# A DoRA linear layer on one core: the loads of blocks 0 and 4 cut into more pieces, and the multiplication by m moved ahead of the sum of squares

## The chip, the cores and the metric

The kernel runs on one core of one Trainium2 chip. The metric is the device time of one execution in microseconds (us); lower is better.

## The reference

`x` has 32,768 rows (16 x 2048) of 256 float32 numbers. `W` is 256 x 256, `lora_A` 256 x 16, `lora_B` 16 x 256, `m` has 256 numbers and `scale` is 1.0.

```python
W_adapted = W + scale * (lora_A @ lora_B)
W_norm = np.sqrt(np.sum(W_adapted ** 2, axis=0, keepdims=True) + 1e-8)
W_final = W_adapted / W_norm * m
y = x.reshape(-1, 256) @ W_final
```

Every input row is read once (33.6 MB) and every output row written once (33.6 MB).

## The kernel before, in words

**Units.** The rows are cut into 8 blocks of 4096 rows. A block is a tile of 128 partitions, in which each partition holds 32 consecutive rows of x, 32 KB that lie together in memory. A block has 8 chunks (4 rows of each partition, 512 rows, 4 KB a partition); chunks are numbered g = 0 to 63, and two chunks make a pair, p = 0 to 31. The last block is loaded and stored as two units of half a block each (16 KB a partition).

**Buffers.** There are five buffers of a block each (`x_bufs`). The output of a chunk is written into the place of its input, and stored from there. So blocks 0 to 4 are loaded without waiting, and blocks 5, 6 and 7 only when the stores of blocks 0, 1 and 2 have freed a buffer.

**SyncE (SP)** issues W's load and all loads of x: chunks 0 and 1, chunks 2 to 7, then blocks 1, 2, 3, 4. Then it waits for stores 0, 1 and 2 (L163), issues blocks 5 and 6 and the first half of block 7, waits for store 3 and issues the second half.

**GpSimd (POOL)** makes the identity and then casts x to bf16 pair by pair into two small buffers (L192). Ahead of a pair it waits for the load that the pair begins (L183), ahead of pair 0 also for the squares on VectorE (`dve` at 4), ahead of pair 15 (`REST`) for store 2, and for the transposes that free its buffer.

**TensorE (PE)** first does the preamble: it transposes A (L267), multiplies A and B (L271), sums the squares of the adapted weights down the columns with a matrix of ones (L278), and spreads m over the partitions with a matmul of one row (L283). It transposes pair 0, waits until VectorE has finished `w_final` (`dve` at 8), and releases two output buffers (`room`). Then a loop runs: transpose pair p + 1 (8 instructions, L297), then the products of pair p (2 x 8 matmuls, L311). The products of pair p thus stand behind the transposes of pair p + 1 in PE's order.

**VectorE (DVE)** adds W and the low-rank part, squares the sum (L218), copies m from PSUM (L220), multiplies it in (L223), takes the reciprocal of the norm (L226), makes `w_final` (L229), and then copies each transposed pair from PSUM to SBUF (L233). The wait ahead of L220 is for `pe` at 4, that is for the sums and for m.

**ScalarE (ACT)** loads A, B and m, takes the square root of the sums (L243), and then copies each chunk's product from PSUM to its place in x's buffer (L251). After some chunks it issues stores on its own queue, as a table written by hand says (chunk after which it is issued in brackets): block 0 (22), block 1 (23), the halves of block 2 (24), the first four chunks of block 3 one by one (27, 4 KB a partition), the rest of block 3 and blocks 4 and 5 (47), block 6 (55), and the halves of block 7 (59 and 63).

Of the kernel before, what the change touches and what calls it, by code (L numbers as in the profile page):

```python
# [11 lines left out]
def kernel(  # L12
# [10 lines left out]
    nc = tc.nc  # L23
# [19 lines left out]
    XBUFS = 5  # L43
    CH = DJ // J
# [18 lines left out]
    def sb(name, shape, dtype):  # L63
        return ctx.enter_context(nc.sbuf_tensor(name, shape, dtype))
# [10 lines left out]
    m_row = sb("m_row", [1, OUT], FP32)  # L75
    identity = sb("identity", [P, P], FP32)
    zeros = sb("zeros", [P, P], FP32)
    ones = sb("ones", [P, P], FP32)
# [18 lines left out]
    mb_ps = y_ps[1][:, 2, :]  # L97
# [3 lines left out]

    units = [(b * CH, CH) for b in range(NBLK - 1)]
    units += [(NCH - CH, CH // 2), (NCH - CH // 2, CH // 2)]
    loads = [(0, 2), (2, CH - 2)] + units[1:]
    load_of = {g: n for n, (g0, cnt) in enumerate(loads) for g in range(g0, g0 + cnt)}


# [17 lines left out]
    def sem(name):  # L125
        if name not in sems:
            sems[name] = tc.alloc_semaphore(name)
        return sems[name]
# [50 lines left out]
    ).then_inc(sem("ident"), 1)  # L179
    for p in range(NPR):  # L180
        b, c = divmod(p, PRB)
        if p == 0 or load_of[2 * p - 1] != load_of[2 * p]:
            nc.gpsimd.wait_ge(sem(f"load{load_of[2 * p]}"), 16)  # L183
        if p == 0:


            nc.gpsimd.wait_ge(sem("dve"), 4)
        if p == REST:
            nc.gpsimd.wait_ge(sem(f"store{HALF}"), 16)
        if p >= NXB:  # L190
            nc.gpsimd.wait_ge(sem("turned"), p - NXB + 1)
        nc.gpsimd.tensor_copy(  # L192
            out=xb_bufs[p % NXB][:],
            in_=x_bufs[b % XBUFS][:, 2 * c * J : 2 * (c + 1) * J, :],
        ).then_inc(sem("rounded"), 1)
# [9 lines left out]
    dv = sem("dve")  # L205
# [10 lines left out]
    ).then_inc(dv, 1)  # L216
    nc.vector.wait_ge(dv, 3)
    nc.vector.tensor_mul(out=sq[:], in0=wa[:], in1=wa[:]).then_inc(dv, 1)  # L218
    nc.vector.wait_ge(sem("pe"), 4)
    nc.vector.tensor_copy(out=m_all[:], in_=mb_ps).then_inc(dv, 1)  # L220
    nc.vector.wait_ge(dv, 5)
    for t in range(KC):
        i = nc.vector.tensor_mul(out=wam[:, t], in0=wa[:, t], in1=m_all[:])  # L223
# [3 lines left out]
    nc.vector.wait_ge(dv, 7)  # L227
    for t in range(KC):
        i = nc.vector.tensor_mul(out=w_final[:, t], in0=wam[:, t], in1=rnorm[:])  # L229
    i.then_inc(dv, 1)  # L230
    for p in range(NPR):
        nc.vector.wait_ge(sem("turned"), p + 1)
        nc.vector.tensor_copy(  # L233
# [5 lines left out]
    nc.scalar.wait_ge(dv, 1)  # L239

    nc.scalar.activation(out=warm[:], in_=eps_col[:], func=AF.Sqrt)  # L241
    nc.scalar.wait_ge(sem("pe"), 3)
    nc.scalar.activation(  # L243
        out=norm[:], in_=n2_ps, func=AF.Sqrt, bias=eps_col[:]
    ).then_inc(sem("act"), 1)
# [1 line left out]
    for g in range(NCH):  # L247
        b, c = divmod(g, CH)
# [14 lines left out]
    pe = sem("pe")  # L263
    nc.tensor.wait_ge(sem("ident"), 1)
    nc.tensor.wait_ge(sem("load_a"), 16)
    for t in range(KC):
        i = nc.tensor.transpose(aT_ps[:, t * P : (t + 1) * P], a_nat[:, t, :], identity[:])  # L267
    i.then_inc(pe, 1)
    nc.tensor.wait_ge(dv, 2)
    for t in range(KC):  # L270
        i = nc.tensor.matmul(  # L271
            ab_ps[:, t, :], aT[:, t * P : (t + 1) * P], b_bf[:], start=True, stop=True
        )
    i.then_inc(pe, 1)
    nc.tensor.wait_ge(dv, 4)

    for t in range(KC):
        i = nc.tensor.matmul(  # L278
            n2_ps, ones[:], sq[:, t, :], start=(t == 0), stop=(t == KC - 1)
        )  # L280
    i.then_inc(pe, 1)
    nc.tensor.wait_ge(sem("load_m"), 16)
    nc.tensor.matmul(mb_ps, ones[0:1, :], m_row[:], start=True, stop=True).then_inc(pe, 1)  # L283
    def take(name):

        nc.tensor.sem_inc(sem(name), -1).wait_op(sem(name), 1, "sem-ge")  # L286
# [6 lines left out]
    def turned(p):  # L293
        take("rounded")

        for j in range(2 * J):
            i = nc.tensor.transpose(  # L297
                xt_ps[p % 2][:, j * P : (j + 1) * P],
                xb_bufs[p % NXB][:, j, :].bitcast(FP32),
                identity[:],  # L300
            )
        i.then_inc(sem("turned"), 1)
# [15 lines left out]
            i.then_inc(sem("product"), 1)  # L318

    turned(0)  # L320

    nc.tensor.wait_ge(dv, 8)
    nc.tensor.sem_inc(sem("room"), 2)
    with nc.Fori(0, NPR // 2, 1, engines=[PE], head_slot={PE: 128}):
        turned(1)
        product(0)
# [45 lines left out]
```

## Time and profile before

| | |
|---|---|
| median of 4 runs | 163.5 us (163.13 to 164.72) |
| the profiled execution's own time | 162.79 us |
| its span, from the first to the last instruction | 161.5 us |
| PE, PE weight loads, DVE, ACT, POOL busy | 60%, 52%, 28%, 40%, 39% of the span |
| moved by DMA | 67.42 MB, 418 GB/s in the mean |
| q1 (SP's queue: loads) | 33.82 MB, 49.0% of 16 engines' span |
| q10 (ACT's queue: stores, A, B, m) | 33.59 MB, 48.9% |

Busy shares are means over the whole span. A core has 16 DMA engines, which serve both queues. The page cuts the span into 40 slices of about 4 us, and gives for each slice the busy tenths of every engine, of the DMA, and the clock that TensorE was granted. Rows of the order of time give the start and the length of an instruction or of several in a row (us), the engine, the line, the tiles, and in brackets how long the engine was idle before and what ended that.

### The profile page before, as it was taken

To read this page: it belongs to the slowest core of one execution; us is meant where nothing else is said; L and a number is where in the kernel's file an instruction comes from. 1 tells how busy PE (TensorE), PEld (TensorE's weight loads), DVE (VectorE), ACT (ScalarE), POOL (GpSimd) and SP (SyncE) were. 2 spreads that over 40 slices of the span, in tenths; PEclk is the share of its full clock that TensorE was granted. 3 is DMA by queue.
4 is the path that set the end of the run, shared out by engine and by line. 5 is a ranking of instruction groups with operands and counts; after the bars stand their busy time and mean duration, and the time that the engine had idled before them with its cause. 6 is when DMAs were issued, how large, how long until landed. Compare 5 with 4: busy or idle time off the path is not lost. (4 is left out here: it accounts for less than half of the span.)

```text
span 161.5 us, 2005 instructions
## 1 busy us (share of the span) xinstructions
PE 96.8 (60%) x786; PEld 84.6 (52%) x786; DVE 44.9 (28%) x44; ACT 64.0 (40%) x67; POOL 62.7 (39%) x39
## 2 busy tenths in 40 slices
PE   0490999999999520000299979999999970000000
PEld 0251799999998310000279968989899960000000
DVE  0547335363535300000033633635353500000000
ACT  3010166868675450000026684684768680000000
POOL 1226719676863000000764449479667400000000
PEclk9999999999999975555559999999999999555555
DMA  4999999999999999999999999999999999999994
GB/s 160 465 420 457 406 503 390 406 503 390 398 511 390 390 495 390 416 430 410 442 384 419 429 449 426 407 438 418 436 463 406 471 422 398 473 430 398 430 434 199
DMA packets 3780, 67.42 MB, mean 418 GB/s; under 512 B 561, under 2 KB 578, under 8 KB 1218
## 3 DMA queue, kind: packets, MB, share of 16 engines
q1 hardware_dynamic: 1584, 33.82, 49.0%
q10 hardware_dynamic: 2194, 33.59, 48.9%
q14 instruction: 2, 0.02, 0.0%
HBM read 33.85 MB, written 33.55 MB: 417 GB/s over the span
## 5 line engine op out<-in xcount | busy, mean ns | idle before, releaser
L251 ACT COPY x_sb<-y_ps 128x1024 f32<-128x1024 f32 x64 | 62.1, 1015 | 61.9 <-PE y_ps L311 61.4
L192 POOL CAST xb<-x_sb 128x2048 bf16<-128x2048 f32 x32 | 60.2, 1893 | 62.9 <-DMA out_dram<-x_sb 27.8
L311 PE MATMUL y_ps<-w_final,xt 128*128 128x256 bf16 x512 | 64.8, 281 | 2.8 <-PEq L286 2.7
L233 DVE COPY xt<-xt_ps 128x1024 f32<-128x1024 f32 x32 | 39.2, 1224 | 76.3 <-PE xt_ps L297 76.3
L311 PEld LDWEIGHTS y_ps<-w_final,xt 128*128 128x128 bf16 x512 | 51.4, 101 | 10.8 <-issue 3.7
L297 PE MATMUL xt_ps<-identity,xb 128*128 128x128 f32 x264 | 37.3, 288 | 27.0 <-PEq L286 27.0
L297 PEld LDWEIGHTS xt_ps<-identity,xb 128*128 128x128 f32 x264 | 32.2, 149 | 29.2 <-issue 28.8
L278 PE MATMUL y_ps<-sq,ones 128*128 128x256 f32 x4 | 2.1, 674 | 1.6 <-DVE sq L218 1.6
L267 PE MATMUL y_ps<-identity,a_nat 128*16 128x128 f32 x2 | 0.6, 394 | 3.6 <-DMA a_nat<-in_lora_A_dram 3.6
L243 ACT ACTIVATE norm<-y_ps,eps_col 128x256 f32<-128x256 f32 x1 | 0.5, 473 | 5.2 <-PE y_ps L278 5.2
L278 PEld LDWEIGHTS y_ps<-sq,ones 128*128 128x128 f32 x4 | 1.2, 324 | 2.3 <-DVE sq L218 2.1
L241 ACT ACT_TABLE_LOAD x1 | 1.3, 1283 | 2.4 <-issue 2.4
L198 POOL MEMSET xb<- 128x2048 bf16 x1 | 1.8, 1804 | 0.7 <-PE xt_ps L297 0.7
L267 PEld LDWEIGHTS y_ps<-identity,a_nat 128*16 128x16 f32 x2 | 0.1, 88 | 3.6 <-issue 3.6
L226 DVE RECIPROCAL rnorm<-norm 128x256 f32<-128x256 f32 x1 | 1.7, 1745 | 0.0
L220 DVE COPY m_all<-y_ps 128x256 f32<-128x256 f32 x1 | 0.4, 425 | 3.3 <-PE y_ps L283 3.3
L283 PE MATMUL y_ps<-m_row,ones 1*128 1x256 f32 x2 | 1.2, 710 | 0.0
L209 DVE CAST b_bf<-b_nat 16x256 bf16<-16x256 f32 x1 | 0.3, 281 | 2.8 <-DMA b_nat<-in_lora_B_dram 2.8
L271 PE MATMUL y_ps<-b_bf,aT 16*128 16x256 bf16 x2 | 0.6, 404 | 0.5 <-DVE aT L211 0.5
L214 DVE SCALAR_TENSOR_TENSOR wa<-y_ps,w_nat 128x512 f32<-128x512 f32 x1 | 0.7, 690 | 0.8 <-PE y_ps L271 0.8
L283 PEld LDWEIGHTS y_ps<-m_row,ones 1*128 1x128 f32 x2 | 0.5, 308 | 0.7 <-issue 0.7
L229 DVE TENSOR_TENSOR w_final<-wam,rnorm 128x256 bf16<-128x256 f32 x2 | 0.8, 422 | 0.0
(13 smaller groups left out, 3.3 us busy)
## 6 DMA issues: line engine op xcount, KB each, us to landing
x_sb<-in_x_dram SPq DMA_DIRECT2D x6, 4096.0 KB, 29.1
out_dram<-x_sb ACTq DMA_DIRECT2D x5, 4096.0 KB, 21.3
out_dram<-x_sb ACTq DMA_DIRECT2D x5, 2048.0 KB, 27.9
x_sb<-in_x_dram SPq DMA_DIRECT2D x2, 2048.0 KB, 33.6
x_sb<-in_x_dram SPq DMA_DIRECT2D x1, 3072.0 KB, 11.8
out_dram<-x_sb ACTq DMA_DIRECT2D x4, 512.0 KB, 48.6
x_sb<-in_x_dram SPq DMA_DIRECT2D x1, 1024.0 KB, 5.0
w_nat<-in_W_dram SPq DMA_DIRECT2D x1, 256.0 KB, 2.9
```

The costliest lines, as they stand in the source:

```text
L192: nc.gpsimd.tensor_copy(out=xb_bufs[p % NXB][:], in_=x_bufs[b % XBUFS][:, 2 * c * J : 2 * (c + 1) * J, :],).then_inc(sem("rounded"), 1)
L198: nc.gpsimd.memset(xb_bufs[NPR % NXB][:], 0.0).then_inc(sem("rounded"), 1)
L214: nc.vector.scalar_tensor_tensor(out=wa[:], in0=ab_ps, scalar=float(scale), in1=w_nat[:], op0=ALU.mult, op1=ALU.add).then_inc(dv, 1)
L226: nc.vector.reciprocal(out=rnorm[:], in_=norm[:]).then_inc(dv, 1)
L229: i = nc.vector.tensor_mul(out=w_final[:, t], in0=wam[:, t], in1=rnorm[:])
L233: nc.vector.tensor_copy(out=xt_bufs[p % NXT][:].rearrange("p r t -> p (r t)").bitcast(FP32), in_=xt_ps[p % 2][:],).then_inc(sem("copied"), 1)
L241: nc.scalar.activation(out=warm[:], in_=eps_col[:], func=AF.Sqrt)
L251: nc.scalar.copy(out=x_bufs[b % XBUFS][:, c * J : (c + 1) * J, :], in_=y_ps[g % 2][:]).then_inc(sem("room"), 1)
L278: i = nc.tensor.matmul(n2_ps, ones[:], sq[:, t, :], start=(t == 0), stop=(t == KC - 1))
L283: nc.tensor.matmul(mb_ps, ones[0:1, :], m_row[:], start=True, stop=True).then_inc(pe, 1)
L297: i = nc.tensor.transpose(xt_ps[p % 2][:, j * P : (j + 1) * P], xb_bufs[p % NXB][:, j, :].bitcast(FP32), identity[:],)
L311: i = nc.tensor.matmul(y_ps[h][:, j, :], xt_bufs[p % NXT][:, r : r + P, t], w_final[:, t, :], start=(t == 0 and (j % (J // 2)) == 0), stop ...
```

## The change

- x's loads: block 0 is loaded in three pieces instead of two (chunks 0 and 1, chunks 2 and 3, chunks 4 to 7). Block 4 is loaded as its first five chunks in one piece, and its last three chunks one by one (4 KB a partition). The order of the loads stays.
- POOL waits ahead of a pair for the loads of both of its chunks, since a pair can now lie in two loads.
- On PE the matmul that spreads m comes ahead of the sum of squares. `pe` is at 3 with m and at 4 with the sums, and VectorE (m) and ScalarE (sums) wait accordingly. VectorE's copy of m and the multiplication by it can run while PE sums.
- VectorE's last instruction on `w_final` increments `room` by two itself; PE no longer stops for `w_final` ahead of its loop.

```diff
-    loads = [(0, 2), (2, CH - 2)] + units[1:]
+    loads = [(0, 2), (2, 2), (4, CH - 4)] + units[1 : XBUFS - 1]
+    loads += [((XBUFS - 1) * CH, CH - 3)]
+    loads += [(XBUFS * CH - 3 + c, 1) for c in range(3)] + units[XBUFS:]
...
-        if p == 0 or load_of[2 * p - 1] != load_of[2 * p]:
-            nc.gpsimd.wait_ge(sem(f"load{load_of[2 * p]}"), 16)
+        for g in (2 * p, 2 * p + 1):
+            if g == 0 or load_of[g - 1] != load_of[g]:
+                nc.gpsimd.wait_ge(sem(f"load{load_of[g]}"), 16)
...
-    nc.vector.wait_ge(sem("pe"), 4)
+    nc.vector.wait_ge(sem("pe"), 3)
     nc.vector.tensor_copy(out=m_all[:], in_=mb_ps).then_inc(dv, 1)
...
         i = nc.vector.tensor_mul(out=w_final[:, t], in0=wam[:, t], in1=rnorm[:])
-    i.then_inc(dv, 1)
+    i.then_inc(sem("room"), 2)
...
-    nc.scalar.wait_ge(sem("pe"), 3)
+    nc.scalar.wait_ge(sem("pe"), 4)
     nc.scalar.activation(
         out=norm[:], in_=n2_ps, func=AF.Sqrt, bias=eps_col[:]
...
+    nc.tensor.wait_ge(sem("load_m"), 16)
+    nc.tensor.matmul(mb_ps, ones[0:1, :], m_row[:], start=True, stop=True).then_inc(pe, 1)
     nc.tensor.wait_ge(dv, 4)
     for t in range(KC):
...
             n2_ps, ones[:], sq[:, t, :], start=(t == 0), stop=(t == KC - 1)
...
-    nc.tensor.wait_ge(sem("load_m"), 16)
-    nc.tensor.matmul(mb_ps, ones[0:1, :], m_row[:], start=True, stop=True).then_inc(pe, 1)
...
     turned(0)
-    nc.tensor.wait_ge(dv, 8)
-    nc.tensor.sem_inc(sem("room"), 2)
     with nc.Fori(0, NPR // 2, 1, engines=[PE], head_slot={PE: 128}):
```

## The prediction

> **What bounds the kernel now.** I read first the page's rows over 40 slices, then the DMA queues, then the order of time on PE, POOL, VectorE and ScalarE's queue at the start and at the hand-over from loads to stores, and last the granted clock in short windows.
>
> ```profile
> span 161.5 us, 2005 instructions
> PEclk9999999999999975555559999999999999555555
> DMA  4999999999999999999999999999999999999994
> q1 hardware_dynamic: 1584, 33.82, 49.0%
> q10 hardware_dynamic: 2194, 33.59, 48.9%
> ```
>
> The DMA row is full in 38 of 40 slices, and the two queues together hold 97.9% of 16 engines' span. So the end is set by the work that the 16 DMA engines have, plus any moment in which they have none; the compute engines (PE 60%) matter only where they leave the DMA without work. The profiled execution took 162.79 us, 1.3 us more than its span; the median of the four runs shown, 163.5, lies 0.7 above it.
>
> There is one place where the DMA depends on the compute. Five blocks are loaded without a pause; the loads end at 51.7 to 52.06 us by the trace's packet records, and the next work is the first store, issued after chunk 22 is evicted:
>
> ```profile
> 13.72 3.75 POOL L192 CAST xb<-x_sb 128x2048 bf16<-128x2048 f32 x2 [4.81 <-DMA x_sb<-in_x_dram]
> 23.43 5.64 POOL L192 CAST xb<-x_sb 128x2048 bf16<-128x2048 f32 x3 [3.76 <-DMA x_sb<-in_x_dram]
> 26.07 1.04 PE L297 MATMUL xt_ps<-identity,xb 128*128 128x128 f32 x8
> 48.98 1.01 ACT L251 COPY x_sb<-y_ps 128x1024 f32<-128x1024 f32 x1 [0.69 <-PE y_ps L311]
> 50.10 0.37 ACTq L145 DMA_DIRECT2D out_dram<-x_sb  x1
> ```
>
> The store is issued at 50.10 and its first packets start at 51.68, 1.58 us later: just as the loads run out. Three engines then needed 2.0 to 2.3 us for their first 32 KB store packet instead of 1.21. The hand-over has no slack; each us that chunk 22 comes later is a us of empty DMA. Chunk 22 hangs on a chain from the load of block 1: it lands at 23.4, pair 4 is cast by 25.3, and PE, which is busy all the time by then, turns pair 4 at 26.07, 0.75 us after it could have. From there PE takes 2.62 us a pair, while a block of four pairs lands every 9.75 us (2.44 a pair), so what PE loses it doesn't get back before chunk 22.
>
> After the hand-over there is cover: four MB of stores are still queued when block 5's loads are released, and the last store is issued at 133.6 while the DMA works to 161.1.
>
> **The change, part by part.**
>
> *Descriptors.* The packet records give one packet per partition row, eight a transfer on each engine: 1213 ns for 32 KB, 912 for 24 KB, 611 for 16 KB, 309 for 8 KB, 159 for 4 KB, 9 for a transfer's completion. Block 4 goes from one 32 KB row to one of 20 KB (midway, 762) and three of 4 KB: 8 x (762 + 3 x 159 - 1213) = 0.21 us for each engine. Block 0: 8 x (309 + 611 - 912) = 0.06. Four more completions: 0.04. Together 0.30 us, in full on the path, since the engines are never free. The 4 KB price is uncertain, because the trace has only 4 KB stores: 159 ns beside 32 KB loads and for the first five or so in a row, but 305 ns for some 45 of them between 81.7 and 83.1 us, just before block 5's loads join. If all 24 per engine took 305, it would be 24 x 0.146 = 3.5 us more. A gain below 159 has no row (2 KB loads take 84, which is 168 for 4 KB). I take 159: the nearest row for loads, eight 2 KB rows of W in succession, shows no such step after its first packet.
> [...]
>
> *Four more issues on SP.* 14 instead of 10, 0.43 us each, all but the last four before SP's long wait; one more lies ahead of block 1's issue, covered by block 0's 4 MB (9.7 us) in the queue. Uncovered, it would be 0.4 us of empty DMA. Block 1 lands when it did, plus 0.1.
>
> *The loads beside the stores.* Should the stores be early, the engines alternate, and each 4 KB load packet lets one 1213 ns store packet pass: 24 x 1.37 = 33 us, so chunks 37 to 39 land by some 84 us instead of 52. POOL's new wait stands before pair 18's cast (86.38 now), with all later casts behind it, and PE, VectorE and ScalarE behind those. It costs nothing, and if it were some us late, the 27 us between the last store's issue and its end would take it.
>
> *m earlier, w_final earlier.* PE's matmul for m (1.22 us at 8.94) moves ahead of the sums, into 5.4 to 6.6, where PE waits for the squares (6.94). m's last packet starts at 5.13, so m may be there a little late; up to 0.3 us could be pushed onto the sums. VectorE then copies m (0.42) and multiplies it in (0.76) from 6.9 to 8.1 instead of 10.20 to 11.4. The square root ends at 9.52, the reciprocal (1.75) at 11.3, w_final (0.76) at 12.1 instead of 13.87: 1.8 us earlier. Moving room's increment to VectorE takes PE's stop for w_final away from pair 1's transposes.
>
> *Block 0 in three.* Pair 1 waited until 13.72 for 3 MB. With 1 MB it lands some 2.4 us after the first load (6.4), at 8.9, as pair 0's cast ends. So pair 0 turns from 9.05, pair 1 from 11.0, and product 0 starts at 13.4 (w_final 12.1, pair 0's copy 1.23) instead of 17.50. Pairs 2 and 3 are cast from 13.8.
>
> So PE is 4 us ahead, and where does that go? Nothing of it reaches the DMA until pair 4, which still can't be cast before 25.3: the head start that counts is the 0.75 us of lateness above. In between PE has products 0 to 2 and pairs 2 and 3 to turn, done at 22 to 23.5, and then stands idle for 2 to 3.3 us. That is what I take to decide the case, because of PE's clock:
>
> ```profile
> 17.50 3.49 PE L311 MATMUL y_ps<-w_final,xt 128*128 128x256 bf16 x16
> 20.83 1.04 PE L297 MATMUL xt_ps<-identity,xb 128*128 128x128 f32 x8
> 21.71 1.91 PE L311 MATMUL y_ps<-w_final,xt 128*128 128x256 bf16 x16
> 58.00:60.00 2.00, 0.07 (x1) 0.00 (x0) 0.00 (x0) 1.01 (x1) 0.00 (x0) 0.57 0.95 410
> 85.00:86.00 1.00, 1.00 (x8) 1.00 (x7) 0.00 (x0) 0.79 (x1) 0.00 (x0) 0.71 0.96 410
> ```
>
> The first and third rows are the same 16 matmuls at the slow and at the full clock (pairs 5.06 and 2.62 us apart); the column before the last two is the granted clock. It rose at 20.7, 5 us after PE became steadily busy, fell at about 58.3, rose at 85.6 (5.8 us after work resumed) and fell at 136.8. These points lie on a grid of 3.41 us (27.3 is 8 steps, 51.2 is 15). It fell at 58.3 although PE had worked 1.44 of the last 3.41 us (42%); it stayed up where a 1.28 us gap left 63%. With a gap of 2 to 3.3 us at 22 to 25.4, most positions of the grid leave one step under half busy, so the clock falls, and PE works pair 4 onward slowly for 3.4 to 6 us. Slow time loses 1 - 2.62/5.06 = 48%: 1.6 to 3.0 us, less the 0.75 gained: chunk 22 comes 0.9 to 2.2 us later than in the profile. I went pair by pair through the order in the code at several positions of the grid; the middle is near the low end, 1.1 us. Of it 0.3 is absorbed, since the loads end 0.3 later, and 0.1 by the overlap of load ends: 0.7 us of empty DMA.
> [...]
>
> Sum against the profiled execution: 162.79 + 0.30 + 0.7 = 163.8. The kernel before has the same lottery: were its clock to rise one grid position later than 20.7, up to 3 us of slow time, its chunk 22 would be up to 1.5 us later, and its median is 0.7 above the profile. So I compare medians: 163.8 with 163.5, 0.2%.
>
> **The rivals.**
>
> *The clock stays up (0.24).* Then the store is issued near 49.4, 0.75 earlier, its packets run among the last 4 KB loads, and no engine is ever empty: 162.79 + 0.30 = 163.1, or 162.9 without the slow first store packets. For it: only part of the positions give a gap in one step. Against it: the row at 58.3.
>
> *The 4 KB loads stall (0.08), the slower side.* Place: 48 to 52 us, 24 packets an engine at 305 ns, 3.5 us: 166.6 with the cover above complete, since the late stores then find the loads still running. It is over 1% once 11 of 24 stall. For it: those 45 packets; against: they stand in one short stretch, and hundreds of others took 159.
>
> *A long slow stretch (0.08).* The clock stays low for two steps or more and chunk 22 is 2.5 to 3 us late: 162.79 + 0.3 + 2.4 = 165.5.
>
> *The label isn't what happens.* In my forecast the 4 KB loads end before the first store packet, so nothing runs beside anything: part of the 0.56 that I give the forecast.
>
> *Faster by over 1% (0.04)* needs 1.6 us less DMA work or gaps. The trace shows no gap of that size to remove; only runs such as the slowest before (164.72) have that much to lose.
>
> **How the numbers follow.** One per cent, 1.6 us, is about what a measurement of this kernel tells from no change. Forecast 163.8, covering 163.4 to 164.6, has 0.56. Faster by over 1%: 0.04. Slower: the stall, and half of the long stretch: 0.12. Within: 0.84. The range 162.8 to 165.4 takes in the covered hand-over and most of the long stretch, and leaves out the stall.
>
> **What would show it.** In the profile after: w_final near 12.1; product 0 near 13.4; pair 4's cast still near 23.5; before it an idle PE of 2 to 3 us, and after it 16 matmuls in 3.5 us rather than 1.9; the first store's issue after 50.1; 4 KB loads of 159 ns. It is wrong if the first store is issued before 50 (the clock held), if the 4 KB loads take 305, or if the DMA row shows a hole elsewhere.

## The result, and the profile after

| | before | after |
|---|---|---|
| median | 164.22 us (162.73 to 165.71, 63 runs) | 163.07 us (162.22 to 165.6, 42 runs) |
| runs below 162.85 / above 163.9 | 2 / 35 | 20 / 7 |
| profiled execution: own time, span | 162.79, 161.5 | 162.27, 161.0 |

The ratio after to before is 0.9941, 95% interval 0.9921 to 0.996: 0.6% faster, where +0.2% was forecast; the time itself lies in the range given. (The ratio leaves out runs over 1.5% above their kernel's fastest; the medians are over all runs.) The four runs known beforehand, median 163.5, had shown the kernel before too well: with 63 runs it is 164.2.

The page's rows of the kernel after (span; granted clock and DMA in 40 slices; the two queues' packets, MB and share):

```profile
span 161.0 us, 2011 instructions
PEclk9999699999999995555569999999999997555555
DMA  4999999999899999989999999999999999999996
q1 hardware_dynamic: 2160, 33.82, 49.3%
q10 hardware_dynamic: 2194, 33.59, 48.9%
```

The DMA still fills the span, and the loads' share has risen from 49.0% to 49.3%: the cost of the smaller descriptors. The dent of the clock in the fifth slice doesn't mean that the clock is lower there than before. The clock's records in these traces begin with its first rise, and the page shows 9 for what lies ahead of it. In the kernel before the first rise stands at 20.7, and product 0 took 3.49 us at the slow clock although its slice shows a 9. Here the clock rises at 11.9, falls at 15.3 and rises again at 18.75. Now the order of time of the kernel after, at the start and at the hand-over:

```profile
7.01 3.92 POOL L197 CAST xb<-x_sb 128x2048 bf16<-128x2048 f32 x2 [5.33 <-DVE sq L223]
...
7.95 3.25 DVE L229 TENSOR_TENSOR wam<-wa,m_all 128x256 f32<-128x256 f32 x2
...
12.90 0.76 DVE L235 TENSOR_TENSOR w_final<-wam,rnorm 128x256 bf16<-128x256 f32 x2
...
15.09 3.37 PE L318 MATMUL y_ps<-w_final,xt 128*128 128x256 bf16 x16 [2.55 <-PEq L293]
18.26 1.28 PE L304 MATMUL xt_ps<-identity,xb 128*128 128x128 f32 x8
19.38 1.91 PE L318 MATMUL y_ps<-w_final,xt 128*128 128x256 bf16 x16
...
25.53 1.06 PE L304 MATMUL xt_ps<-identity,xb 128*128 128x128 f32 x8 [1.62 <-PEq L293]
...
49.59 0.37 ACTq L149 DMA_DIRECT2D out_dram<-x_sb  x1
```

Two casts now run back to back from 7.0. The multiplication by m beside them takes 3.25 us, not 0.76, so w_final is ready at 13.66, only 0.2 earlier than before. Product 0 starts at 15.09 instead of 17.50 all the same, since pair 1's transposes were done early. Product 1, at 19.38, runs at the full clock. PE waits 1.62 us ahead of pair 4 and comes out of it at the full clock, and the first store is issued at 49.59, 0.5 us earlier than in the profile before.

Between these two profiles the hand-over gains nothing by a hole: in neither was the DMA empty. Their ends differ by the last DMA engine, which finishes at 160.44 instead of 161.09, while the median engine finishes at 159.48 and 159.40. The gain in the medians has to come from executions that these two don't show.

### The profile page after: what moved, and what is told of

It is laid out like the page before. It is cut to its first block, busy times and chain, and to the rows that moved or that the text cites. A ratio compares the mean times of both kernels' runs of the same rounds, so it can differ in the third digit from the quotient of the medians.

```text
span 161.0 us, 2011 instructions
## 1 busy us (share of the span) xinstructions
PE 95.6 (59%) x786; PEld 84.0 (52%) x786; DVE 47.3 (29%) x44; ACT 64.0 (40%) x67; POOL 62.7 (39%) x39
## 3 DMA queue, kind: packets, MB, share of 16 engines
q1 hardware_dynamic: 2160, 33.82, 49.3%
## 5 line engine op out<-in xcount | busy, mean ns | idle before, releaser
L304 PE MATMUL xt_ps<-identity,xb 128*128 128x128 f32 x264 | 36.7, 285 | 25.6 <-PEq L293 25.6
L229 DVE TENSOR_TENSOR wam<-wa,m_all 128x256 f32<-128x256 f32 x2 | 3.3, 1664 | 0.0
```

The lines of the kernel that those rows point to most:

```text
L304: i = nc.tensor.transpose(xt_ps[p % 2][:, j * P : (j + 1) * P], xb_bufs[p % NXB][:, j, :].bitcast(FP32), identity[:],)
```

## The experiments

Theory H (hand-over): the time is the DMA's work plus what a late first store costs, and it is PE's clock, which differs from execution to execution, that makes the store late. Rivals: the gain is in the DMA's own work (D, the small loads of block 4), or in w_final (M). A hole is a time in which DMA engines have nothing to move. The time "beside" a run is that of the kernel before on the same chip.

### Does a late first store cost time, and an early one save it?

Stores of blocks 0 and 1 after chunk 24 (kernel before otherwise):

```diff
-    stores = [(b * CH, CH, 22 + b) for b in range(F - 1)]
+    stores = [(b * CH, CH, 24) for b in range(F - 1)]
```

> The kernel before, with the stores of blocks 0 and 1 issued after chunk 24, as block 2's halves are. H: the first store comes 2.6 us later (two chunks at 1.31 us), and all of it is empty DMA: medians 2.4 to 2.8 us above the kernel before, a hole of 2 to 3 us near 52 us in the trace. If the hand-over has slack, or the end is set elsewhere, the time rises by less than 1 us.

Measured: 164.89 (4 runs), the kernel before beside it 162.99; ratio 1.0118 (1.0086 to 1.015). The windows of this run (DMA share and GB/s in the last two columns):

```profile
50.00:52.00 2.00, 2.00 (x21) 1.84 (x20) 1.22 (x1) 1.31 (x3) 0.06 (x1) 1.00 0.65 279
52.00:53.60 1.60, 1.60 (x17) 1.53 (x15) 0.23 (x1) 0.64 (x1) 0.00 (x0) 1.00 0.00 0
53.60:56.00 2.40, 0.61 (x6) 0.29 (x4) 1.00 (x1) 0.05 (x1) 0.00 (x0) 1.00 1.04 437
```

No packet starts for 1.6 us. The store was issued at 52.75 and its first packet starts at 53.62: 0.87 us from issue to packet on empty engines, not the 1.58 that the prediction read from the profile before. There the packet had been waiting behind the last loads, so that profile held about 0.7 us of slack more than I had counted. That fits the 1.9 us that 2.65 us of delay cost, though a second cost of a late store, told below, is in these 1.9 us as well.

One chunk later (`23 + b`):

> The kernel before, with the stores of blocks 0 and 1 issued after chunks 23 and 24: 1.0 us later. By the prediction's step (no slack at the hand-over, 1.58 us from issue to packet) every run is 1.0 us longer, the fastest near 163.7. By the trace with the stores after chunk 24 (0.87 us from issue to packet once the DMA is empty) there is about 1 us of slack: the fastest runs stay at 162.3 to 162.9, and only runs with a late chunk 22 gain up to 1.0.

Measured: 165.22 beside 163.99; ratio 1.0071 (1.0035 to 1.0107), fastest run 163.66. Neither expectation fits the whole: the typical run pays the full us, and the fastest pays more than the slack should let through. Its profile (164.58) shows one run that had no slack left. PE's order of time:

```profile
18.51 3.62 PE L311 MATMUL y_ps<-w_final,xt 128*128 128x256 bf16 x16
21.93 1.34 PE L297 MATMUL xt_ps<-identity,xb 128*128 128x128 f32 x8
23.11 1.91 PE L311 MATMUL y_ps<-w_final,xt 128*128 128x256 bf16 x16
24.85 1.04 PE L297 MATMUL xt_ps<-identity,xb 128*128 128x128 f32 x8
```

The start of the kernel before, with nothing changed in it but the store: the clock rises within the 21.93 row (22.5) instead of at 20.7, and pair 3 is turned at 24.85 instead of 23.45. Those 1.4 us stay, and with the chunk's us the store is issued at 52.41. Its first packet starts 0.88 us later, and the packet records show 1.48 us of empty DMA in the mean over the engines.

Earlier instead (`20 + b`) in the kernel before:

> The kernel before, with the stores of blocks 0 and 1 issued after chunks 20 and 21 instead of 22 and 23; nothing else. H: the first store is queued some 2.6 us before the loads run out, so the DMA is never empty: a median of 162.3 to 162.9 and hardly any spread upward, against 164.2 with a spread to 165.7. D or M: the hand-over is not the matter, 164.2, or slower if the early stores hold up block 4's loads.

Measured: 163.21 (162.26 to 163.48, 12 runs) beside 164.57 (to 166.12); ratio 0.993 (0.9896 to 0.9964). The upward scatter is gone with this one number, as H says, but the median isn't at the floor: loads that run when the stores come in are slowed (32 KB packets of up to 2.8 us near 49.6; 1.0 us more than the usual durations from 45 to 60 us, in the mean over the engines).

The same in the changed kernel, twice, and one chunk early (`21 + b`):

> The changed kernel with the stores of blocks 0 and 1 issued after chunks 20 and 21. H: no empty DMA in any run, 162.2 to 162.7 with a spread below 0.5. It also tells what the 4 KB loads are worth beside stores: with 32 KB loads and early stores the median was 163.2 and loads of 1.2 us took up to 2.8 us while the stores came in. If 4 KB loads mend that, this one lies 0.5 to 1 us below; if not, at 163.2.

> The changed kernel with the stores of blocks 0 and 1 issued after chunks 20 and 21, again, on a chip where the kernel before scatters. Hole: none above 163.3, median near 162.8 (as on the other chip: loads and early stores together cost some tenths). Lag of the last engine: the changed kernel's scatter.

> The changed kernel with the stores of blocks 0 and 1 issued after chunks 21 and 22, one chunk earlier. If the hole makes the slow runs: the first store is issued 1.3 us earlier in every run, runs up to 1.3 us late lose their hole, so nearly all at 162.3 to 163.0, at most one or two above 163.5, median 162.6 or less. If the last engine's lag makes them: the changed kernel's scatter, 162.2 to 165.6, median 163.1.

Measured: 162.84 (162.43 to 163.05) beside 162.99 (ratio 0.9988, 0.9966 to 1.001) on a chip where the kernel before did not scatter above 163.6; then 162.88 (162.68 to 163.28) with `20 + b` and 162.89 (162.35 to 163.58) with `21 + b`, beside 164.31 (to 165.79). Ratios of the last two: 0.9926 (0.9891 to 0.9961) and 0.9937 (0.9907 to 0.9967). With the store early the scatter falls away, as in the kernel before, so it is the late store's. (The changed kernel itself was not run beside them.) The rival in the last two, the engine that finishes last, is left with the 0.6 and 1.2 us over which these runs spread. It isn't nothing: two executions with the usual stores took 163.42 and 163.53 (the profiles of "m and room alone" and of the second run with extra matmuls, below) without a hole, and their last engine finishes at 161.60 and 161.70.

What these traces also show is that a late store costs twice. When block 5's loads come in, near 81 us, packets are slowed; the sum above the usual durations from 75 to 90 us, in the mean over the engines, is 0.21 us in the profile after, 1.07 in an execution with a late store (below), and 0.00 to 0.04 with early stores. Over all 20 profiles it grows with the time at which the first store is issued: 0.09 to 0.39 for 49.0 to 49.9 us, 0.48 and 0.50 for 50.1 (0.50 is the profile before), 0.77 for 50.68 (block 4 split alone, without a hole), 1.02 to 1.09 from 51.3 on. So half a us of the store's time went with 0.3 us between the two profiles above, about what the smaller descriptors cost, though no engine was ever empty. Why these packets are slowed was not tried.

### Which part of the change does it?

Block 0 in three loads alone:

```diff
-    loads = [(0, 2), (2, CH - 2)] + units[1:]
+    loads = [(0, 2), (2, 2), (4, CH - 4)] + units[1:]
```

> The kernel before, with block 0 in three loads and nothing else of the change. Theory H (hand-over): the time is the DMA's work, about 162.3 to 162.8 us, plus the moment in which the DMA has nothing between the last load of block 4 and the first store, and chunk 22 sets that moment. Pair 1 is then cast at 8.9 instead of 13.7, products start near 15 (w_final at 13.9), and pair 4 is no longer late behind its load: most of the gain, a median of 163.0 to 163.5 against 164.2 before. Theory M (the gain is w_final's): no gain, 164.2. Theory D (the gain is in the DMA's own work, by the small loads of block 4): 164.2.

Measured: 163.39 (162.18 to 163.98) beside 164.57; ratio 0.9966 (0.993 to 1.0002), as H expects in the median, at the edge of what the interval tells. From a run's span and mean clock one can work out where its clock's last fall stood on the grid of 3.41 us (slow stretches between a fall and the next rise are whole steps at a granted clock of 0.50: 27.31 us, or 8 steps, in the profile before, 3.41 and 23.89 us, or 1 and 7, in the profile after; so it is span x (2 x clock - 1), modulo 3.41). Sorted by that, the nine runs from 0.5 to 2.7 us rise almost without exception from 163.07 to 163.98: same code, same chip, and the time goes with the position of the grid. The position alone doesn't settle it: in the kernel before on this chip a run at 1.49 took 164.59 and one at 1.53 took 163.71. What else differs between such runs stays open.

Block 4 split alone (`units[1 : XBUFS - 1]`, then five chunks and three single ones, with POOL's double wait):

> The kernel before, with block 4 as five chunks and three single ones and nothing else. H: chunk 22 comes as before; the loads end 0.2 us later, which takes 0.2 us from the empty moment where there is one and adds 0.2 to the work: 164.2, within 0.3 of the kernel before. D: the whole gain, 163.1. M: 164.2.

Measured: 164.44 (162.42 to 165.83) beside 164.57; ratio 0.9925 (0.9874 to 0.9976). The medians of all runs say no change, while the ratio says faster: not conclusive by itself. Taking the split out of the changed kernel tells more:

> The changed kernel, with block 4 in one load of 32 KB rows as before. H: the split of block 4 does nothing for the hand-over but lengthen the loads by 0.2 us, so this is within 0.3 us of the changed kernel (163.1), and its fastest runs 0.2 faster (162.0). If the split is what brings the gain: 164.2 or more.

> The changed kernel with block 4 in one load, once more, beside the changed kernel on one chip. H: the same groups, and the fastest runs up to 0.2 below those of the changed kernel. If the 4 KB loads cover a late first store, the changed kernel's slow group is nearer to its fast one than here.

> The changed kernel once more, beside the others on one chip. H: two groups, 162.2 to 162.8 where the clock holds, and 163.0 to 165.6, rising with the position of the clock's grid, where it falls before pair 4.

Measured: first 162.24 (162.15 to 163.14, 6 runs) beside 162.99 (ratio 0.9964, 0.994 to 0.9989). Then, on one chip, 162.99 (162.31 to 165.24) without the split and 163.11 (162.23 to 165.86) with it, beside 163.99; ratios 0.9949 (0.9908 to 0.999) and 0.9943 (0.9898 to 0.9987). The split is worth nothing that can be measured; D falls.

m and room alone, all loads as before:

> The kernel before, with m spread ahead of the sums and multiplied in early (and room released by VectorE) and block 0 and 4 loaded as before. H: pair 1 still lands at 13.7, and the products of pair 0 stand behind its transposes, so nothing moves: 164.2, within 0.3. M: the gain, 163.1. The profile should also tell whether the multiplication by m (0.38 us an instruction before, 1.66 after) is slow because POOL casts at the same time: in this kernel pair 0's cast ends at 8.9 and only the first of the two should be slow.

Measured: 163.26 (162.63 to 163.88) beside 164.57; ratio 0.9934 (0.99 to 0.9969). H had expected nothing here, and was wrong. Its profile has products from 17.63 and a first store at 50.09, like the profile before, so M doesn't explain it either: an earlier w_final didn't bring earlier products. The gain is that no run of the 12 lies above 163.9; how the earlier sums bring that about, these traces don't tell. It did answer its side question (VectorE, then POOL):

```profile
7.99 1.58 DVE L224 TENSOR_TENSOR wam<-wa,m_all 128x256 f32<-128x256 f32 x2
```

```profile
7.06 1.89 POOL L192 CAST xb<-x_sb 128x2048 bf16<-128x2048 f32 x1 [5.38 <-DVE sq L218]
```

With one cast beside it instead of two, ending at 8.95, the pair of multiplications takes 1.58 us, and without any 0.76.

### What makes chunk 22 late: a clock that rises late (R), or one that falls in the gap before pair 4 (F)?

Block 1 in two halves, so that pair 4 needn't wait (changed kernel, block 4 whole):

```diff
-    loads = [(0, 2), (2, 2), (4, CH - 4)] + units[1 : XBUFS - 1]
...
+    loads = [(0, 2), (2, 2), (4, CH - 4)]
+    loads += [(CH, CH // 2), (CH + CH // 2, CH // 2)] + units[2:]
...
```

> The changed kernel with block 4 in one load again and block 1 in two halves (chunks 8 to 11, 12 to 15). H with the clock: pair 4 can then be cast at about 18.5 instead of 23.5, PE has no gap of 1.6 us or more ahead of it, its clock doesn't fall there, and chunk 22 comes 1 to 1.5 us earlier than in the kernel before, limited by block 2's landing. So nothing above 162.8, median 162.1 to 162.4, on a chip where the changed kernel and the kernel before scatter upward. If the clock's fall before pair 4 isn't what makes the slow runs of the changed kernel, this one scatters as it does.

Measured: 163.59 (162.34 to 164.78) beside 163.99; ratio 0.998 (0.9944 to 1.0017). It scatters like the others, so by its own expectation the fall before pair 4 is not what makes the late runs, or not alone.

Four matmuls that only keep PE busy, in the kernel before:

```diff
     turned(0)
+    for n in range(4):
+        nc.tensor.matmul(xt_ps[1][:, 0:OUT], ones[:], sq[:, 0, :], start=True, stop=True)
```

> The kernel before, and four matmuls of 128x128 by 128x256 in float32 more on PE, right behind pair 0's transposes, into a buffer that pair 1 overwrites; they do nothing but keep PE busy where it waited for pair 1 (12.1 to 15.8 us). H with the clock: the clock rises before the first products, chunk 22 comes at its load's pace, 0.7 us earlier than in the profile before, and the runs above 164 vanish: median 162.4 to 163.2. If the clock isn't what scatters the runs: as before, 164.2 to 164.6.

> The kernel before with four matmuls more that keep PE busy behind pair 0's transposes, once more, on another chip. R: the clock has risen before the first products in every run, so nothing above 163.3 where the kernel before scatters to 165.5; median 162.4 to 163.0. F: the gap of 1.7 us before pair 4, which this kernel has and the kernel before has not, brings runs of 164 and more.

Measured: 162.73 (162.29 to 163.12) beside 162.99, ratio 0.9984 (0.996 to 1.0009); on the other chip 163.39 (162.58 to 165.38) beside 164.34, ratio 0.996 (0.9913 to 1.0007). Both profiles show what was meant: the first products take 1.91 us instead of 3.49, and the first store is issued at 49.48 and 49.54. But runs above 164 remain, five of 12, so a late rise is not all. (The second profile took 163.53 without a hole; its last engine finishes at 161.70.)

The same in the changed kernel with block 4 whole, with block 1 whole and in halves, and the changed kernel beside them:

> The changed kernel with block 4 in one load, and the same four matmuls behind pair 0's transposes. Products 0 to 2 then run at the full clock and end near 22.5, so the gap before pair 4 is about 3 us. R: the gap does no harm, all runs at 162.2 to 162.9. F: the clock falls in the gap in most runs, chunk 22 is 1 to 2 us late, median 163.5 or more, with a trace that shows the slow clock from 24 to 30.

> As the one before, and block 1 in two halves, which takes the gap before pair 4 away. R and F both: all runs at 162.2 to 162.7, since neither the late rise nor the fall is left, and the first store is issued near 48.6. If it scatters to 164 like the kernels without the extra matmuls, the clock at the start isn't the cause and both theories fall.

> The changed kernel once more, beside these on one chip: two groups again, 162.2 to 162.8 and 163.0 to 165.6. If its profile falls in the upper group, R expects a clock that rises at 22 or later and no fall before pair 4; F a fall between 22 and 27.

Measured beside 164.34: 164.0 (162.54 to 165.69, ratio 0.9995, 0.9951 to 1.0038); 163.1 (162.3 to 165.88, ratio 0.9954, 0.9911 to 0.9998); the changed kernel 162.55 (162.28 to 165.67, ratio 0.9933, 0.9892 to 0.9975). The first is F's number, and its profile (163.38) shows the clock fall at 25.7 and rise at 29.1, after 3.36 us without work:

```profile
25.60 1.87 PE L299 MATMUL xt_ps<-identity,xb 128*128 128x128 f32 x8 [3.36 <-PEq L288]
...
27.26 2.81 PE L313 MATMUL y_ps<-w_final,xt 128*128 128x256 bf16 x16
```

And the changed kernel's profile this time is the execution that the prediction described (163.70). Its order of time, then its windows, in which the granted clock is the third column from the end:

```profile
25.83 1.06 PE L304 MATMUL xt_ps<-identity,xb 128*128 128x128 f32 x8 [3.37 <-PEq L293]
26.73 3.35 PE L318 MATMUL y_ps<-w_final,xt 128*128 128x256 bf16 x16
29.88 1.30 PE L304 MATMUL xt_ps<-identity,xb 128*128 128x128 f32 x8
...
51.55 0.37 ACTq L149 DMA_DIRECT2D out_dram<-x_sb  x1
```

```profile
25.00:27.00 2.00, 1.17 (x11) 1.16 (x12) 0.07 (x1) 0.00 (x0) 2.00 (x2) 1.00 1.21 524
27.00:30.00 3.00, 3.00 (x17) 2.14 (x15) 1.16 (x1) 1.01 (x1) 2.36 (x2) 0.50 0.91 393
30.00:31.00 1.00, 1.00 (x9) 1.00 (x8) 0.00 (x0) 0.88 (x1) 0.00 (x0) 0.79 0.91 393
```

Here the clock rose early (13.4), products 0 to 2 went at full speed, PE stood for 3.37 us, and the clock fell at 27.0 for one step of the grid. Store 0 goes out 1.96 us later than in the other profile of the same kernel, the DMA is empty for 0.29 us, and the execution is 1.43 us longer. So R and F both exist: R in a profile with the start of the kernel before, F in two with the changed start. But the kernel with halves and the extra matmuls still has three runs of 12 above 164, and by its expectation both theories fall as the whole cause. In its profile (162.35) PE, ahead of the loads, waits 2.75 us before block 2's first pair (that cast starts at 33.43, and product 6 ends at 32.7), so the gap may only have moved; no profile of a late run of it exists to show a fall there. No execution above 163.70 with the usual store table was profiled, of any kernel here. That the store is late in those of 164 and more is inferred from the early stores, which took them away; what makes it late there isn't shown.

## Why the prediction was wrong

**What was right.** The bound (the DMA, with one place where it hangs on the compute). The descriptors' 0.30 us: the last load packet ends at 52.33 instead of 52.06, the 4 KB loads took 159 to 172 ns, and the 305 ns stall did not come. (The row for that stall was over-counted: 29 packets from 81.7 to 83.1 took 240 ns or more, not some 45.) No cost from SP's issues or from POOL's waits. Pair 4 as the gate, and the gap before it. The clock's fall in that gap and a time of 163.8: there is an execution with the fall, a first store at 51.55 and 163.70.

**The step that failed: which of the executions is the likely one, in both kernels.** The forecast gave the fall, with 0.7 us of empty DMA, the largest chance, and 0.24 to a clock that stays up. In the profile after, the clock stays up in the gap, the first store is issued at 49.59 (the prediction's own sign that it is wrong) and the empty DMA is 0. Of the 42 runs 20 are below 162.85, where every profiled execution has its first store at 50.1 or earlier. For the kernel before it was said that its clock might rise up to 3 us later and its store be 1.5 us late, and the profile with 22.5 shows a rise 1.8 us later and a store 1.4 us late; but its median, 163.5, was taken from four runs, and over half of the 63 lie above 163.9 (median 164.22). A reading of the same mechanism that fits is that the kernel before, whose products begin at 17.5 at the slow clock and never catch up, is late more often than the changed one, which starts them at 15.1. The runs show that it is longer more often; that this is the reason is argued, not shown.

**Terms that were mis-sized.** The first is the gap before pair 4: it was put at 2 to 3.3 us and is 1.62 in the profile after (3.37 in the other one), with 52% of the grid's step busy, above the 42% at which the clock had fallen. One cause is the second term: w_final was put at 12.1 and came at 13.66. Beside POOL's casts the two multiplications by m took 1.22 and 2.11 us, against 0.42 each without a cast in the profile before, and the second ended at 11.2, after the cast's end at 10.93. With one cast beside them the pair took 1.58 (m and room alone). Why they are slower there isn't shown. Moving VectorE work beside POOL's casts had been costed at its price alone. The matmul for m also started only at 6.24, when m had come, and pushed the sums from 6.94 to 7.39, 0.45 us instead of up to 0.3. The third is the hand-over: 0.87 us from issue to packet instead of 1.58, so 0.7 us more of slack; and a late store costs more in a second place (1.07 us instead of 0.21 near 81 us) than in the hole (0.29) that alone was counted. With the stores after chunk 20 the 4 KB loads end at 66.7 and 65.4 us, not at 84: about 11 of the 24 on each engine were left when the first store packet started, and these went at about the 1.37 us reckoned. The rival with the clock up was priced at 163.1, and the profile after is 162.27: the slowed packets near 81 us are 0.29 us less than before, and the last engine ends 0.96 instead of 1.69 us behind the median one. No term of the forecast had the latter; that it came out so in this pair of profiles is luck.

**When the clock fell.** The prediction went by the row at 58.3, where the clock fell though PE had worked for 42% of the 3.41 us before. The later traces bear that out. The fall at 25.7 (extra matmuls, block 4 whole) ends a step of the grid that was nearly without work (22.3 to 25.7). The fall at 27.0 (the changed kernel's profile of 163.70) ends a step, 23.6 to 27.0, in which PE worked from 25.83 on: 1.17 us, or 34%; the gap of 3.37 us ahead of it lies in two steps and fills neither. In the profile after it fell at 15.3, where the gap was 2.55 us and 25% of the step was busy. After the 1.62 us without work ahead of pair 4, with 52% of the step busy, the clock stayed up. Whether the work in a step is what decides, these traces don't show.

## What to carry to other kernels

When the times of a kernel spread by more than the effect sought, ask first what differs between its executions; a profile of one of them, and a median of four, can't say which is typical. Where a queue must be fed in time, give the feeding work slack instead of speed: issuing the first stores one or two chunks earlier took the scatter away with one number (worst of 24 runs 163.58, against 165.6 to 165.9 in the changed kernel's three sets of runs, which were not taken beside these), though it isn't shown to be faster than the changed kernel in the ratio. And read the latency of a transfer from one that found its engines empty, not from one that queued (0.87 us from issue to packet against 1.58 here).

## What was not expected of the hardware

- 32 KB loads took up to 2.8 us instead of 1.21 while stores came in beside them (stores early), which no row of the kernel before had shown.
- One of the 16 DMA engines finishes last in nearly every profile without a hole (160.4 to 161.7 us, the median engine mostly between 159.3 and 160.2); its 32 KB store packets take about 1.28 us instead of 1.21 between 117 and 140 us. That moves the end by about a us between executions. Its cause was not tried.
- The kernel before had a median of 162.99 on one chip and 163.99 to 164.57 on four others. A kernel's time says little without the kernel before on the same chip.
